# The samples' share of the last 256 features, their statistics and their output moved behind the second tokens' last product

## The chip, the cores and the metric

The kernel runs on one NeuronCore of one Trainium2 chip. The metric is the device time of one launch in microseconds (us), and a lower one is better. Engines are named as the profile names them: PE is TensorE (PEld its weight loads), DVE is VectorE, ACT is ScalarE, POOL is GpSimd, SP is SyncE, which here only issues transfers.

## The reference

One layer of a decoder trunk is computed for 256 prompt tokens and for 32 sample tokens (8 sequences of 4), with 2048 features, in float32. The part that matters here is its end: the feed-forward block, and a layer norm over the 2048 features of each token.

```python
    x = layer_norm(ALPHA * x + merged @ w_o, ln1_g, ln1_b)
    hid = jnp.square(jax.nn.relu(x @ w_up))
    x = layer_norm(ALPHA * x + hid @ w_down, ln2_g, ln2_b)

def layer_norm(x, g, b):
    xf = x.astype(jnp.float32)
    mu = jnp.mean(xf, -1, keepdims=True)
    var = jnp.mean(jnp.square(xf - mu), -1, keepdims=True)
    return ((xf - mu) * lax.rsqrt(var + LN_EPS) * g.astype(jnp.float32) + b.astype(jnp.float32)).astype(x.dtype)
```

The last `x` is written out as `y_prompt` (256 x 2048) and `y_sample` (32 x 2048).

## The kernel before

**Layout and blocks.** All activations lie with features on the 128 partitions and the 288 tokens along the free axis: columns 0 to 127 are the first prompt tokens, 128 to 255 the second, 256 to 287 the samples. A weight matrix is cut into blocks of 512 KB. For each, SP loads the block (`raw`), ACT rounds it to a high part (`hi`, L184), DVE subtracts for the low part (`lo`, L139), and PE multiplies both with the split activations (L216, L218). The loop `for i in range(len(blocks))` writes all engines' programs in one order by hand. The tile framework adds the semaphore waits between engines. Functions that belong to a block's end are hung on a later block by `at(i, f)`.

**The last 256 features.** The last product, `hid @ w_down`, adds up in `acc`. Its last 256 features (the four blocks from `mark["end"]` on) are made the other way round, with tokens on partitions: `products` (L747) writes them for the first 128 tokens into `T0[:, 256:512]` and for the second 128 into `T1`. `T0` and `T1` lie in the first halves of PSUM tiles of two times 512 columns (`acp`, two buffers). Into both, the residual is turned by products with the identity.

**The samples.** Their features are put in four groups of 32 partitions and 512 columns, `sg2`. Three quarters and more come out of `acc`: `sample_copy` (ACT, L679) gathers them, and `sample_turn` (PE, L683) turns them. The share of the last 256 features is made by `sample_products` (L701): sixteen float32 products of the samples' hidden values `hs32` with the raw weights, which leave four partial sums in a PSUM tile of its own. ACT copies them out (`s4`, L704), and one product with the constant `sel96` (L761) adds the four up in `sg2[:, 256:512]`. Then come `sample_stats` (DVE `bn_stats`, L687), four small copies that bring the groups' figures to the same 32 partitions (L714), `bn_aggr`, root, reciprocal and four copies back (`sample_means`, L726 to L730), two DVE passes over 128 x 512 (`Ys`, L142), and four transfers `y_sample` (L814). Before, `sample_products` stands ahead of the block `mark["end"] - 1`, the turning of the last groups and L761 at the start of `first_tokens`, the statistics in `late_tiles` and `sample_means`, and the `y_sample` transfers ahead of the first tokens' statistics in `final`.

**The second tokens' end.** After the last product into `T1`, PE turns three units of 512 features out of `acc` into the tiles `ws` (L841), while DVE and ACT make mean and root of the second tokens (L843 to L850). `to_rows` turns the two figures into rows (L805, L806), and `rank` (L809) adds a six-row product to each unit, so that one multiplication by 1/root finishes it. ACT does that for the units 0 and 1 (L863), DVE for unit 2 (L861). The transfers are L776: SP issues those of the units 0 and 2, ACT that of unit 1.

Of the kernel before, what the change touches and what calls it, by code (L numbers as in the profile page):

```python
# [9 lines left out]
F32 = mybir.dt.float32  # L10
# [91 lines left out]
def hybrid_kernel(ctx: ExitStack, tc: tile.TileContext, A):  # L102
# [16 lines left out]
    def nm(s):  # L119
        counter[0] += 1  # L120
        return f"{s}{counter[0]}"

    def gtile():
        n = nm("g")
        return gp.tile([P, 512], F32, tag="g", name=n)
# [15 lines left out]
    def stt(out, a, s, b, o0, o1):  # L141
        dve.scalar_tensor_tensor(out=out, in0=a, scalar=s, in1=b, op0=o0, op1=o1)  # L142
# [439 lines left out]
    def down_evac(c, p):  # L582
        def f(ps):
            a = ph["acc"][:, 2 * p:2 * p + 2, :]
            tt(a, a, ps[:, :, 0:NT], ADD)
        if c == 3:
            idle = lambda ps: None
            if p == 0:
                return [f, idle, lambda ps: out_tiles(p)]
            if p in (2, 5):  # L590
                u = p // 3
                return [f, lambda ps: out_tiles(p), lambda ps: block_stats(u, range(4)),
                        lambda ps: (block_stats(u, range(4, 8)), block_rows(u), block_moves(u, (0, 1)))] + (
                            [idle] * (3 * u)) + [lambda ps: block_moves(u, (2, 3))]
            if p == 6:
                return [f, late_tiles, lambda ps: sample_means(0), lambda ps: sample_means(1)]
            gain = lambda ps: tt(ph["Y"][:, 0, 0:512], ph["Y"][:, 0, 0:512], ph["g2"][:, 0:512], MUL)
            return [f, lambda ps: tail_rows(p // 2), lambda ps: out_tiles(p)] + [gain] * (p == 4)
        return [f]
# [81 lines left out]
    def sample_turn(w0, first):  # L681
        for w in (w0, w0 + 1):
            pe.matmul(ph["sg2"][:, w * P:w * P + P], ph["cs"][:, w * P:w * P + P], ident,  # L683
                      start=not first or w == w0, stop=not first, is_transpose=True)

    def sample_stats(u):
        dve.bn_stats(out=ph["bns"][:, u, :], in_=ph["sg2"][:, 256 * u:256 * u + 256])  # L687
# [7 lines left out]
        sample_copy(3)  # L695

    def sample_products():
        s4 = gtile()
        for k in range(KT):
            w = k % 4  # L700
            pe.matmul(s4[32 * w:32 * w + 32, 0:256], ph["hs32"][:, k, :], raw[mark["end"] + k // 4][:, w, :],  # L701
                      start=k < 4, stop=k >= KT - 4)
        ph["s4"] = ph["pool"].tile([P, 2, NT], F32, tag="yt", name="s4", bufs=2)[:, 0, 0:256]
        act.copy(ph["s4"], s4[:, 0:256])  # L704

    def late_tiles(ps):
        sample_turn(0, False)
        for u in range(2):
            sample_stats(u)
        a, sm, T0 = ph["acc"], ph["sm"], ph["T0"]  # L710
        for k in range(2):
            pe.matmul(T0[:, k * P:k * P + P], a[:, 12 + k, 0:P], ident, start=False, stop=False, is_transpose=True)
        for j in range(4):
            (act.copy if j % 2 else gps.tensor_copy)(ph["bnq"][:, j], ph["bns"][32 * j:32 * j + 32].rearrange("p k s -> p (k s)"))  # L714
        g = gtile()
        for k in range(2):
            pe.transpose(g[:, k * P:k * P + P], a[:, 12 + k, P:NP_], ident)
        dve.bn_stats(out=ph["bn"][:, 1, 8, :], in_=g[:, 0:256])
        act.copy(ph["Y"][:, 1, 1536:1792], g[:, 0:256])


    def sample_means(step):
        sm = ph["sm"]
        mq, mr = sm[0:32, 20:22], sm[:, 22:24]
        if step == 0:
            dve.bn_aggr(out=mq, in_=ph["bnq"])  # L726
            act.activation(mq[:, 1:2], mq[:, 1:2], AF.Sqrt, bias=epsc[0:32, 0:1])
            dve.reciprocal(out=mq[:, 1:2], in_=mq[:, 1:2])
            for j in range(4):
                (act.copy if j % 2 else gps.tensor_copy)(mr[32 * j:32 * j + 32], mq)  # L730
            return
        fin, bn = ph["fin"], ph["bn"]
        for b, n in ((0, 8), (1, 9)):
            dve.bn_aggr(out=fin[:, b, 1:3], in_=bn[:, b, 0:n])
            dve.tensor_scalar(out=fin[:, b, 2:3], in0=fin[:, b, 2:3], scalar1=fin[:, b, 0:1], scalar2=None, op0=MUL)
        stt(ph["Ys"], ph["sg2"], mr[:, 0:1], ph["gs"], SUB, MUL)

    kept = []

# [9 lines left out]
    def first_tokens(i, k0):  # L749
        kept.append((his.pop(i), los.pop(i)))  # L750
        a = ph["acc"]
        if k0 == 0:
            ph["T0"] = acp.tile([P, 2, 512], F32, tag="acc", name=nm("acc"))[:, 0]
            for k in range(2):
                pe.matmul(ph["T0"][:, 256 + k * P:256 + k * P + P], a[:, 14 + k, 0:P], ident,
                          start=k == 0, stop=False, is_transpose=True)
            sample_copy(0)
            sample_copy(1)
            ph["sg2"] = gtile()
            sample_turn(2, True)  # L760
            pe.matmul(ph["sg2"][:, 256:512], cst("sel96"), ph["s4"], start=False, stop=True)  # L761
        products(ph["T0"][:, 256:512], 0, k0 // KB)

    def final():
        a, fin, sm, Y, Ys = ph["acc"], ph["fin"], ph["sm"], ph["Y"], ph["Ys"]
        g2, b2 = ph["g2"], ph["b2"]
        T0 = ph["T0"]
        T1 = acp.tile([P, 2, 512], F32, tag="acc", name=nm("acc"))[:, 0, 0:256]
        for k in range(2):
            pe.matmul(T1[:, k * P:k * P + P], a[:, 14 + k, P:NP_], ident, start=k == 0, stop=False, is_transpose=True)  # L770
        for j in range(2):
# [37 lines left out]
            pe.matmul(w, ph["st5"][b], ph["m5"][:, 512 * n:512 * n + 512], start=start, stop=True)  # L809


        stt(Ys, Ys, sm[:, 23:24], ph["bs"], MUL, ADD)
        for j in range(4):
            sp.dma_start(A["y_sample"].rearrange("b t f -> (b t) f")[:, 512 * j:512 * j + 512], Ys[32 * j:32 * j + 32])  # L814

        c = slice(1536, D)
        dve.bn_stats(out=fin[:, 0, 3:9], in_=T0)
        dve.bn_aggr(out=sm[:, 0:2], in_=fin[:, 0])
# [16 lines left out]
        finish_unit(0, 0, w)  # L835
        finish_unit(0, 2)

        ws = [gtile() for _ in range(3)]
        for n, w in enumerate(ws):
            for k in range(4):  # L840
                pe.matmul(w[:, P * k:P * k + P], a[:, 4 * n + k, P:NP_], ident, start=(k == 0), stop=False,  # L841
                          is_transpose=True)
        dve.bn_stats(out=fin[:, 1, 3:9], in_=T1)  # L843
        dve.bn_aggr(out=sm[:, 2:4], in_=fin[:, 1])
        root(1)
# [1 line left out]
        high(1, mv)  # L847
        centred(1, slice(1792, D), T1)
        low(1, mv)
        dve.reciprocal(out=sm[:, 7:8], in_=sm[:, 3:4])  # L850
        for c in (slice(1792, D), slice(1536, 1792)):
            if c.start == 1536:
                centred(1, c, Y[:, 1, c])
            stt(Y[:, 1, c], Y[:, 1, c], sm[:, 7:8], b2[:, c], MUL, ADD)
            out(1, 3, c=c)
        to_rows(1)
        for n in (0, 2, 1):
            c = slice(512 * n, 512 * n + 512)
            rank(ws[n], 1, n, False)
            if n == 2:  # L860
                dve.tensor_scalar(out=Y[:, 1, c], in0=ws[n], scalar1=sm[:, 7:8], scalar2=None, op0=MUL)  # L861
            else:
                act.mul(Y[:, 1, c], ws[n], sm[:, 7:8])  # L863
            out(1, n, act if n == 1 else sp)

    mark["up"] = len(blocks)
    for c in range(4):
# [818 lines left out]
    for i in range(len(blocks)):  # L1686
# [71 lines left out]
            tail_consts()  # L1758
        if i == mark["end"] - 3:
            sample_sum()  # L1760
        if i == mark["end"] - 1:
            sample_products()
        matmuls(i)
        if i == 4:
            x_last()
# [47 lines left out]
```

## Time and profile before

| what | us |
|---|---|
| median of 3 runs (lowest, highest) | 1650.9 (1650.72, 1651.02) |
| the profiled execution, its own time | 1650.88 |
| its span, first instruction to the end of the last | 1649.1 |
| PE busy | 1642.1 |
| DVE, ACT, POOL busy | 987.3, 780.2, 136.6 |
| PE's share of the chain that ended last | 98% |

The span is what the trace shows; 1.78 us of the execution's own time lie outside it. PE is busy nearly all the time, and the chain that ended last runs through PE up to the last product into `T1`. Behind that it hops between DVE, ACT and PE, and the last transfers follow. Idle time of any other engine costs nothing by itself, unless PE or this tail waits for it.

### The profile page before, as it was taken

What the parts mean: (1) busy time and instruction counts of PE and PEld (TensorE: products, weight loads), DVE (VectorE), ACT (ScalarE), POOL (GpSimd) and SP (SyncE); (2) the same over time, 40 slices, a digit from 0 to 9 for tenths busy, and PEclk for the clock granted to TensorE, in tenths of its full rate; (3) what the DMA queues carried; (4) which work ended last, traced back from release to release, by engine and by line L of the source; (5) the groups of instructions that cost most, each with busy time, mean ns of one, the idle gap of its engine ahead of it and who ended that gap; (6) DMA issues with size and microseconds to landing.
All of it is one profiled execution on the core that took longest, in us unless ns stands there. A gap on an engine that the chain in (4) does not pass through costs nothing.

```text
span 1649.1 us, 30934 instructions
## 1 busy us (share of the span) xinstructions
PE 1642.1 (100%) x12858; PEld 1629.3 (99%) x12858; DVE 987.3 (60%) x1342; ACT 780.2 (47%) x1216; POOL 136.6 (8%) x286
## 2 busy tenths in 40 slices
PE   9999999999999999999999999999999999999998
PEld 8999999999999999999999999999999999999998
DVE  6787788878544444457776666444444444444466
ACT  7774678367533333334354454443334433344354
POOL 1132214234000000000000000000000000000111
PEclk9999999999999999999999999999999999999999
DMA  8667466846655555555565555555555555555653
GB/s 266 174 176 207 141 173 199 226 117 185 191 166 166 167 166 167 167 166 160 178 202 166 168 166 167 166 165 165 164 164 164 165 165 166 167 166 167 181 164 100
DMA packets 278999, 282.49 MB, mean 171 GB/s; under 512 B 15075, under 2 KB 272920, under 8 KB 278596
## 3 DMA queue, kind: packets, MB, share of 16 engines
q1 hardware_dynamic: 274394, 268.42, 54.2%
q0 software_dynamic: 4032, 11.63, 2.5%
q8 instruction: 101, 1.65, 0.4%
q10 hardware_dynamic: 432, 0.46, 0.1%
q14 instruction: 40, 0.33, 0.1%
HBM read 272.83 MB, written 7.63 MB: 170 GB/s over the span
## 4 chain that ended last, share of the span: by engine, by line
PE 98%; ACT 0%; DVE 0%; POOL 0%; issue 0%; ACTq 0%
PE acc L216 63%; PE acc L218 31%; PE acc L747 1%; PE g L1541 0%; PE g L1561 0%; PE g L1564 0%; PE g L1341 0%; PE g L1241 0%; PE g L1514 0%; PE g L1553 0%; PE g L1350 0%; PE g L1045 0%; PE g L701 0%; PE g L1425 0%; PE g L1402 0%; DVE lo L139 0%
## 5 line engine op out<-in xcount | busy, mean ns | idle before, releaser
L139 DVE TENSOR_TENSOR lo<-raw,hi 128x1024 fp32r<-128x1024 f32 (+1 forms) x503 | 607.1, 1210 | 561.0 <-ACT hi L184 558.6
L184 ACT CAST hi<-raw 128x1024 fp32r<-128x1024 f32 (+1 forms) x499 | 518.8, 1042 | 725.3 <-PE acc L216 637.5
L216 PE MATMUL acc<-xh,hi 128*128 128x288 f32 x1408 | 397.4, 298 | 0.0
L216 PE MATMUL acc<-xl,hi 128*128 128x288 f32 x1408 | 393.9, 295 | 0.0
L218 PE MATMUL acc<-xh,lo 128*128 128x288 f32 x1408 | 302.0, 295 | 0.1
L216 PE MATMUL acc<-dl,hi 128*128 128x288 f32 (+1 forms) x1024 | 287.7, 295 | 0.0
L216 PE MATMUL acc<-dh,hi 128*128 128x288 f32 (+1 forms) x1024 | 287.4, 295 | 0.0
L216 PE MATMUL acc<-hl,hi 128*128 128x288 f32 x992 | 277.8, 295 | 0.0
L216 PE MATMUL acc<-hh,hi 128*128 128x288 f32 x992 | 277.4, 294 | 0.0
L216 PEld LDWEIGHTS acc<-xh,hi 128*128 128x128 f32 x1408 | 264.4, 188 | 2.6 <-issue 1.3
L216 PEld LDWEIGHTS acc<-xl,hi 128*128 128x128 f32 x1408 | 264.2, 188 | 0.7
L218 PEld LDWEIGHTS acc<-xh,lo 128*128 128x128 f32 x1408 | 225.9, 188 | 0.4 <-DVE lo L139 0.3
L218 PE MATMUL acc<-dh,lo 128*128 128x288 f32 (+1 forms) x1024 | 219.8, 296 | 0.0
L218 PE MATMUL acc<-hh,lo 128*128 128x288 f32 x992 | 213.2, 296 | 0.0
L216 PEld LDWEIGHTS acc<-dh,hi 128*128 128x128 f32 x1024 | 193.3, 189 | 0.0
L216 PEld LDWEIGHTS acc<-dl,hi 128*128 128x128 f32 x1024 | 192.8, 188 | 0.0
L216 PEld LDWEIGHTS acc<-hh,hi 128*128 128x128 f32 x992 | 186.4, 188 | 0.4 <-issue 0.4
L216 PEld LDWEIGHTS acc<-hl,hi 128*128 128x128 f32 x992 | 186.1, 188 | 0.0
L218 PEld LDWEIGHTS acc<-dh,lo 128*128 128x128 f32 x1024 | 164.5, 188 | 0.0
L218 PEld LDWEIGHTS acc<-hh,lo 128*128 128x128 f32 x992 | 159.0, 188 | 0.0
L216 PE MATMUL acc<-mh,hi 128*128 128x288 f32 x256 | 71.9, 297 | 0.0
L216 PE MATMUL acc<-ml,hi 128*128 128x288 f32 x256 | 71.7, 295 | 0.0
(425 smaller groups left out, 1475.4 us busy)
## 6 DMA issues: line engine op xcount, KB each, us to landing
raw<-in_w_in_dram SPq DMA_DIRECT2D x175, 512.0 KB, 3.9
raw<-in_w_up_dram SPq DMA_DIRECT2D x128, 512.0 KB, 3.8
raw<-in_w_down_dram SPq DMA_DIRECT2D x128, 512.0 KB, 3.5
raw<-in_w_o_dram SPq DMA_DIRECT2D x32, 512.0 KB, 3.6
raw<-in_w_a_out_dram SPq DMA_DIRECT2D x16, 512.0 KB, 3.6
raw<-in_w_b_out_dram SPq DMA_DIRECT2D x16, 512.0 KB, 3.6
out_dram<-S POOLq DMA_DIRECT2D x8, 512.0 KB, 4.5
S<-in_state_gdn_dram POOLq DMA_DIRECT2D x4, 512.0 KB, 6.4
```

The source lines that it names most:

```text
L139: dve.tensor_tensor(out=out, in0=a, in1=b, op=op)
L184: act.copy(his[i][:, k:k + step], raw[i][:, k:k + step])
L216: pe.matmul(o, h[:, k, c], x, start=st and x is xh_, stop=False)
L218: pe.matmul(o, l[:, k, c], xh_, start=False, stop=en)
L747: pe.matmul(out, x[:, kk, c], w[:, k, :], start=False, stop=stop)
```

## The change

The sixteen products of the samples with the raw weights (L700 in the changed file) now follow the last product into `T1`. Their partial sums go into the second half of `T1`'s tile (`ph["s4p"]`), and `sg2` is the second half of `T0`'s tile, where both had PSUM tiles of their own. All four `sample_turn` products stand together in `late_tiles`. ACT copies the partial sums between two steps of the second tokens' statistics. The three units of the second tokens are turned one by one just ahead of their `rank`, the `sel96` product stands in unit 0, and ACT multiplies all three. The samples' statistics stand between unit 0 and unit 2, their small copies are shared by DVE and POOL instead of ACT and POOL, and the `y_sample` transfers come last.

```diff
@@ down_evac @@
             if p == 6:
-                return [f, late_tiles, lambda ps: sample_means(0), lambda ps: sample_means(1)]
+                return [f, late_tiles, lambda ps: None, lambda ps: earlier_records()]
@@ sample_products @@
-        s4 = gtile()
         for k in range(KT):
             w = k % 4
-            pe.matmul(s4[32 * w:32 * w + 32, 0:256], ph["hs32"][:, k, :], raw[mark["end"] + k // 4][:, w, :],
+            pe.matmul(ph["s4p"][32 * w:32 * w + 32], ph["hs32"][:, k, :], raw[mark["end"] + k // 4][:, w, :],
                       start=k < 4, stop=k >= KT - 4)
         ph["s4"] = ph["pool"].tile([P, 2, NT], F32, tag="yt", name="s4", bufs=2)[:, 0, 0:256]
-        act.copy(ph["s4"], s4[:, 0:256])
@@ late_tiles @@
         sample_turn(0, False)
-        for u in range(2):
-            sample_stats(u)
+        sample_turn(2, True)
+        sample_stats(0)
...
-        for j in range(4):
-            (act.copy if j % 2 else gps.tensor_copy)(ph["bnq"][:, j], ph["bns"][32 * j:32 * j + 32].rearrange("p k s -> p (k s)"))
...
-    def sample_means(step):
+    def sample_mean(step):
         sm = ph["sm"]
         mq, mr = sm[0:32, 20:22], sm[:, 22:24]
         if step == 0:
+            sample_stats(1)
+            for j in range(4):
+                (dve if j < 2 else gps).tensor_copy(ph["bnq"][:, j], ph["bns"][32 * j:32 * j + 32].rearrange("p k s -> p (k s)"))
             dve.bn_aggr(out=mq, in_=ph["bnq"])
+        elif step == 1:
             act.activation(mq[:, 1:2], mq[:, 1:2], AF.Sqrt, bias=epsc[0:32, 0:1])
             dve.reciprocal(out=mq[:, 1:2], in_=mq[:, 1:2])
             for j in range(4):
-                (act.copy if j % 2 else gps.tensor_copy)(mr[32 * j:32 * j + 32], mq)
-            return
+                (dve if j < 2 else gps).tensor_copy(mr[32 * j:32 * j + 32], mq)
+            stt(ph["Ys"], ph["sg2"], mr[:, 0:1], ph["gs"], SUB, MUL)
+            stt(ph["Ys"], ph["Ys"], mr[:, 1:2], ph["bs"], MUL, ADD)
+
+    def earlier_records():
         fin, bn = ph["fin"], ph["bn"]
...
-        stt(ph["Ys"], ph["sg2"], mr[:, 0:1], ph["gs"], SUB, MUL)
@@ first_tokens @@
-            ph["T0"] = acp.tile([P, 2, 512], F32, tag="acc", name=nm("acc"))[:, 0]
+            t0 = acp.tile([P, 2, 512], F32, tag="acc", name=nm("acc"))
+            ph["T0"], ph["sg2"] = t0[:, 0], t0[:, 1]
...
-            ph["sg2"] = gtile()
-            sample_turn(2, True)
-            pe.matmul(ph["sg2"][:, 256:512], cst("sel96"), ph["s4"], start=False, stop=True)
@@ final @@
-        T1 = acp.tile([P, 2, 512], F32, tag="acc", name=nm("acc"))[:, 0, 0:256]
+        t1 = acp.tile([P, 2, 512], F32, tag="acc", name=nm("acc"))
+        T1, ph["s4p"] = t1[:, 0, 0:256], t1[:, 1, 0:256]
...
-        stt(Ys, Ys, sm[:, 23:24], ph["bs"], MUL, ADD)
-        for j in range(4):
-            sp.dma_start(A["y_sample"].rearrange("b t f -> (b t) f")[:, 512 * j:512 * j + 512], Ys[32 * j:32 * j + 32])
...
-        ws = [gtile() for _ in range(3)]
-        for n, w in enumerate(ws):
-            for k in range(4):
-                pe.matmul(w[:, P * k:P * k + P], a[:, 4 * n + k, P:NP_], ident, start=(k == 0), stop=False,
-                          is_transpose=True)
+        sample_products()
         dve.bn_stats(out=fin[:, 1, 3:9], in_=T1)
...
         low(1, mv)
+        act.copy(ph["s4"], ph["s4p"])
+        to_rows(1)
...
-        to_rows(1)
-        for n in (0, 2, 1):
+
+        def unit(n):
+            w = gtile()
+            for k in range(4):
+                pe.matmul(w[:, P * k:P * k + P], a[:, 4 * n + k, P:NP_], ident, start=(k == 0), stop=False,
+                          is_transpose=True)
+            if n == 0:
+                pe.matmul(ph["sg2"][:, 256:512], cst("sel96"), ph["s4"], start=False, stop=True)
             c = slice(512 * n, 512 * n + 512)
-            rank(ws[n], 1, n, False)
-            if n == 2:
-                dve.tensor_scalar(out=Y[:, 1, c], in0=ws[n], scalar1=sm[:, 7:8], scalar2=None, op0=MUL)
-            else:
-                act.mul(Y[:, 1, c], ws[n], sm[:, 7:8])
+            rank(w, 1, n, False)
+            act.mul(Y[:, 1, c], w, sm[:, 7:8])
             out(1, n, act if n == 1 else sp)
+
+        unit(0)
+        sample_mean(0)
+        sample_mean(1)
+        unit(2)
+        unit(1)
+        for j in range(4):
+            sp.dma_start(A["y_sample"].rearrange("b t f -> (b t) f")[:, 512 * j:512 * j + 512], Ys[32 * j:32 * j + 32])
@@ the loop over the blocks @@
-        if i == mark["end"] - 1:
-            sample_products()
```

The order in which instructions stand, first on PE between the first and the second of the four last blocks (`acc_17693` and `acc_17674` are `T0`'s tile, `g_17698` is `sg2` before, `r` holds the gathered samples, `cf` the identity). Before:

```order
L747 MATMUL acc_17693<-hi_17545,hl_15798 128x256
L683 MATMUL g_17698<-cf,r_16693 128x128 x2
L712 MATMUL acc_17693<-cf,acc 128x128 x2
L717 MATMUL g_17724<-cf,acc 128x128 x2
L747 MATMUL acc_17693<-hi_17581,hh_15797 128x256
```

The same place in the changed kernel:

```order
L749 MATMUL acc_17674<-hi_17545,hl_15798 128x256
L683 MATMUL acc_17674<-cf,r_16693 128x128 x4
L710 MATMUL acc_17674<-cf,acc 128x128 x2
L713 MATMUL g_17698<-cf,acc 128x128 x2
L749 MATMUL acc_17674<-hi_17581,hh_15797 128x256
```

All four turned groups now stand here, and they go into the same tile as the products around them. In the built program the wait of L710 for DVE counts up to the `bn_stats` of that tile (L687); before, the wait of L712 counted up to the last addition into `acc`.

PE from the last product into `T1` on (`acc_17785` and `acc_17751` are `T1`'s tile, the three `g` tiles of L841 and L855 the units). Before:

```order
L747 MATMUL acc_17785<-hi_17688,hl_15798 128x256
L841 MATMUL g_17865<-cf,acc 128x128 x4
L841 MATMUL g_17866<-cf,acc 128x128 x4
L841 MATMUL g_17867<-cf,acc 128x128 x4
L805 MATMUL g_17892<-cf,R 6x128
L809 MATMUL g_17865<-g_16692 128x512
L809 MATMUL g_17867<-g_16692 128x512
L809 MATMUL g_17866<-g_16692 128x512
```

The changed kernel, behind the same last product:

```order
L700 MATMUL acc_17751<-raw_17446,hs_17553 32x256 x4
L700 MATMUL acc_17751<-raw_17480,hs_17553 32x256 x4
L700 MATMUL acc_17751<-raw_17511,hs_17553 32x256 x4
L700 MATMUL acc_17751<-raw_17543,hs_17553 32x256 x4
L806 MATMUL g_17850<-cf,R 6x128
L855 MATMUL g_17859<-cf,acc 128x128 x4
L858 MATMUL acc_17674<-s_17842,g_14818 128x256
L810 MATMUL g_17859<-g_16692 128x512
L855 MATMUL g_17882<-cf,acc 128x128 x4
L810 MATMUL g_17882<-g_16692 128x512
L855 MATMUL g_17890<-cf,acc 128x128 x4
L810 MATMUL g_17890<-g_16692 128x512
```

The sixteen products stand where the twelve turns stood, and the turns stand behind L806. They write `T1`'s tile, and in the built program the wait of the second tokens' `bn_stats` (L843 before, L836 now) for PE counts up to the last instruction that wrote this tile: the last L747 before, the last L700 now.

ACT from the second tokens' root (L791, now L792) on. Before:

```order
L791 ACTIVATE r_16693<-r_16693,epsc 128x1
L797 COPY R<-r_16693 128x2x2
L806 COPY g_16692<-g_17892 6x128
L863 ACTIVATE Y<-g_17865,r_16693 128x512
L863 ACTIVATE Y<-g_17866,r_16693 128x512
L776 DMA out_dram<-Y 128x512
```

The changed kernel:

```order
L792 ACTIVATE r_16693<-r_16693,epsc 128x1
L798 COPY R<-r_16693 128x2x2
L843 COPY s_17842<-acc_17751 128x256
L807 COPY g_16692<-g_17850 6x128
L861 ACTIVATE Y<-g_17859,r_16693 128x512
L727 ACTIVATE r_16693<-r_16693,epsc 32x1
L861 ACTIVATE Y<-g_17882,r_16693 128x512
L861 ACTIVATE Y<-g_17890,r_16693 128x512
L777 DMA out_dram<-Y 128x512
```

The samples' root (L727) now stands between the first and the second multiplication of the second tokens.

## The prediction

> **What bounds the kernel now.** The page comes first: the span, PE's busy share, and the chain that ended last.
>
> ```profile
> span 1649.1 us, 30934 instructions
> PE 1642.1 (100%) x12858; PEld 1629.3 (99%) x12858; DVE 987.3 (60%) x1342; ACT 780.2 (47%) x1216; POOL 136.6 (8%) x286
> PE 98%; ACT 0%; DVE 0%; POOL 0%; issue 0%; ACTq 0%
> ```
>
> PE bounds everything up to the last product into `T1`. So an instruction taken off PE ahead of that point is worth its time, and what stands behind it counts only along the tail. The second view is the chain in order of time (start, us, what), around the place that loses the sixteen products, and from the last product on.
>
> ```profile
> 1621.97 1.86 PE g L701 x32
> ...
> 1627.44 0.22 PE g L683 x2
> 1627.65 0.43 PE g L761 x2
> 1628.09 1.42 PE acc L747 x12
> 1629.51 0.22 PE g L683 x2
> 1629.72 0.22 PE acc L712 x2
> ```
>
> ```profile
> 1641.16 0.02 issue
> 1641.18 0.44 DVE r L843
> ...
> 1642.61 0.04 issue
> 1642.65 0.29 PE g L805
> ...
> 1642.96 0.26 ACT g L806
> ...
> 1643.27 0.51 PE g L809
> ...
> 1643.85 0.44 ACT Y L863
> ...
> 1644.43 0.68 ACT Y L863
> ```
>
> The reader sees a tail of 3.95 us from the last product (1641.16) to ACT's last multiplication (1645.11). I count it from S, the start of the second tokens' `bn_stats` (L843), here 1641.18: L805 starts at S+1.47 and ends at S+1.76.
>
> **The stream ahead of the last product: 2.29 us come off PE.** These are the sixteen products (1.86) and the `sel96` product (0.43). The first pair of L683 (0.22) only moves behind the twelve L747. So PE would reach the four L683 at 1629.51 - 1.86 - 0.43 - 0.22 = 1627.00. They turn what ACT copies in L679, and the timeline shows ACT and DVE there (start, us, engine, line, [idle before <- releaser]):
>
> ```profile
> 1625.03 1.44 ACT L674 COPY Y<-Y 32x192 f32<-32x192 f32 x4
> 1626.49 0.37 ACT L704 COPY s<-g 128x256 f32<-128x256 f32 x1
> 1627.03 1.05 ACT L184 CAST hi<-raw 128x1024 fp32r<-128x1024 f32 x1 [0.17 <-ACT s L704]
> 1628.05 0.50 ACT L679 COPY r<-acc 128x128 f32<-128x128 f32 x2
> ...
> 1628.11 1.23 DVE L139 TENSOR_TENSOR lo<-raw,hi 128x1024 fp32r<-128x1024 f32 x1
> 1629.76 0.76 DVE L687 BATCH_NORM_STATS2 r<-g 128x6 f32<-128x256 f32 x2 [0.42 <-PE g L683]
> ```
>
> **The stall that takes most of it back.** ACT is occupied without a gap until L674 ends at 1626.47, and nothing of that depends on PE. With L704 gone, the cast L184 starts at 1626.49 instead of 1627.03, and the two L679 end at 1626.49 + 1.52 = 1628.01. PE therefore waits from 1627.00 to about 1627.85 for the first copy and to 1628.05 for the second, and its fourth L683 is done near 1628.55. Then L710 stands behind L687, since `sg2` now shares `T0`'s tile. DVE does the subtraction L139 first: the cast ends at 1627.54, so L139 runs from 1627.57 to 1628.80, and one L687 (half of 0.76, and up to 0.43) ends near 1629.20. A released pair on PE costs 0.04 + 0.29 + 0.11, by L805's rows and the pipelined half of 0.22, so L710 is through at 1629.64; before, L712 was through at 1629.94. Of 2.29 us 0.30 are left, between 0.1 and 0.5 by how the copies overlap. The last product into `T1` ends at 1641.16 - 0.30 = 1640.86. Here PE idles in two pieces (0.85 and 0.65 us) where before it had none; all that follows it, the first tokens' end included, only moves along.
>
> **The tail: the sixteen products stand ahead of the statistics.** L700 writes into `T1`'s tile, and the `bn_stats` of the second tokens (L836) waits for the last instruction that wrote this tile. So it starts at 1640.86 + 1.86 + 0.02 = 1642.74 = S, 1.56 later than before. What was meant to lie beside the statistics lies ahead of them, and PE idles during them, while the twelve turns that lay there move behind L806 (the old L805).
>
> From there I follow the samples, since their transfers are now last. PE ends L806 at S+1.76, four turns (2 x 0.22) at S+2.20, the `sel96` product (0.43) at S+2.63. ACT's copy of the partial sums fits between its other steps, as ACT's st5 copy (L807) starts only at S+1.78. DVE is occupied longer, by the three L142 over the last 512 features:
>
> ```profile
> 1642.70 1.40 DVE L142 SCALAR_TENSOR_TENSOR Y<-Y,r,g 128x256 f32<-128x256 f32 x3
> ```
>
> That is to 1644.10 before, S+2.92. Then the second L687 ends at S+3.30. The steps that follow it are the old ones, in which DVE takes ACT's copies; the old rows time them:
>
> ```profile
> 1630.59 0.41 POOL L714 COPY r<-r 32x12 f32<-32x12 f32 x2 [3.23 <-DVE r L687]
> 1631.07 0.36 DVE L726 BATCH_NORM_AGGREGATE r<-r 32x2 f32<-32x48 f32 x1 [0.21 <-POOL r L714]
> 1631.46 0.29 ACT L727 ACTIVATE r<-r,epsc 32x1 f32<-32x1 f32 x1 [0.20 <-DVE r L726]
> 1631.79 0.15 DVE L728 RECIPROCAL r<-r 32x1 f32<-32x1 f32 x1 [0.36 <-ACT r L727]
> 1632.00 0.39 POOL L730 COPY r<-r 32x2 f32<-32x2 f32 x2 [1.01 <-DVE r L728]
> 1633.08 0.75 DVE L142 SCALAR_TENSOR_TENSOR r<-g,r,gs 128x512 f32<-128x512 f32 x1
> 1633.86 0.75 DVE L142 SCALAR_TENSOR_TENSOR r<-r,bs 128x512 f32<-128x512 f32 x1
> 1634.64 1.75 SPq L814 DMA_DIRECT2D out_dram<-r  x4
> ```
>
> L687 ended at 1629.76 + 0.76 = 1630.52 and ACT's root began at 1631.46, 0.94 later; so L727 now begins at S+4.24. From there 0.54 to POOL's copies, 0.39 for them, 0.07 to the first pass over `Ys`, 0.78 to the second and 0.75 in it: `Ys` is done at S+6.77. SP starts the first of four transfers 0.03 later (1633.86 + 0.75 to 1634.64), S+6.80, and the fourth 3/4 of 1.75 later, S+8.11 = 1650.85. All of these hops take as long as they did; none is hidden by other work now, where before PE's stream hid them all.
>
> ACT must keep program order: after unit 0's multiplication (rank at about S+3.1, done by S+3.8) comes L727, which waits for DVE until S+4.24. Units 2 and 1 are queued behind it and start only at S+4.55. The two multiplications, 1.26 us together by the old chain (1643.85 to 1645.11), end at S+5.81, and ACT issues its transfer at 1648.58. SP's transfer of unit 2 waits for such a multiplication, and the y_sample transfers stand behind it on SP, but `Ys` is later anyway. Ahead of the first tokens' transfers, where they stood, nothing waited for them: SP's first L776 came at 1637.26, 0.87 after the last had been issued (1634.64 + 1.75). Giving DVE's old multiplication to ACT costs one more 0.6 us there. Before:
>
> ```profile
> 1637.26 8.17 SPq L776 DMA_DIRECT2D out_dram<-Y  x8
> ...
> 1645.03 0.40 SPq L776 DMA_DIRECT2D out_dram<-Y  x1
> 1645.14 0.35 ACTq L776 DMA_DIRECT2D out_dram<-Y  x1
> ```
>
> **The end of the span.** How long it lasts from the last transfer I take from the windows of half a us (engines, granted clock, share of the DMA engines, GB/s), around the old `y_sample` transfers and at the end.
>
> ```profile
> 1636.50:1637.00 0.50, 0.50 (x6) 0.50 (x6) 0.50 (x2) 0.20 (x1) 0.00 (x0) 1.00 0.56 139
> 1637.00:1637.50 0.50, 0.50 (x6) 0.50 (x5) 0.50 (x3) 0.00 (x0) 0.00 (x0) 1.00 0.37 90
> ...
> 1646.50:1647.00 0.50, 0.00 (x0) 0.00 (x0) 0.00 (x0) 0.00 (x0) 0.00 (x0) 0.62 0.99 381
> ...
> 1647.50:1648.00 0.50, 0.00 (x0) 0.00 (x0) 0.00 (x0) 0.00 (x0) 0.00 (x0) 0.50 0.09 29
> ```
>
> The fourth old transfer started at 1634.64 + 1.31 = 1635.95, and the traffic stopped 0.37 / 0.56 of a half us after 1637.00, at 1637.33: 1.38 after the issue. At the end traffic stops at 1647.55, 1.55 ahead of the span's end. So now the data end at 1650.85 + 1.38 = 1652.23 and the span at 1653.8, +4.7 us. ACT's transfer alone, 3.44 us later than before, would end it at 1652.5; its 256 KB are through before the samples' last 64 KB.
>
> **Sum.** From S the old tail took 1649.10 - 1641.18 = 7.92 us, the new one takes 8.11 + 1.38 + 1.55 = 11.04. Span: 1649.10 - 0.30 (stream) + 1.86 (products in the tail) + 3.12 (the longer tail) = 1653.78. The profiled execution's own time was 1650.88, 1.78 above its span and 0.02 under the median 1650.9. So **1655.6 us**, 4.7 or 0.28% over before; 0.2%, about what a measurement can tell from no change, is 3.3 us, at 1654.2. My own bounds: the stall's rest 0.1 to 0.5; DVE's 32-partition copies instead of ACT's, from nothing to 0.3 either way (0.41 for two on POOL is the nearest row, and I take that they end beside POOL's); the transfers' end 0.3 less or 0.5 more. Together 1654.8 to 1656.6.
>
> **Rivals.** *Waits by half tile (0.08).* The two uses of each shared tile lie in different halves of 512 columns. The page "PSUM — Partial Sum Buffer" of the Trainium skill, section "PSUM bank collisions raise a hardware error", asks for a guard per bank and quadrant, and its specifications give 512 float32 values as a bank; no trace here shows it. If waits went by halves, L710 would follow the last L683 at 1628.55, 1.17 earlier than before, so `T1` would end at 1639.99 and the statistics start at S' = 1640.01, beside L700. L700 would end at 1641.85, and L806 at 1642.13, then turns and `sel96` (0.87) at 1643.00, and L687 at 1643.43 instead of S+3.30 = 1646.04. That is 2.6 less: 1653.0, not slower by the 0.2%. It decides from the place of one wait, L836's. Against it speaks the built program, where L836 counts up to the last L700 and L710 up to L687.
>
> *The early stall is smaller (0.05).* If ACT's copies came early enough, the whole 2.29 would be kept though L836 still waits for L700: 1655.6 - 2.0 = 1653.6. Against it: ACT has no gap from 1625.03 to 1628.55.
>
> *The PE clock falls (0.05).* PE's last three products before:
>
> ```profile
> 1643.27 0.96 PE L809 MATMUL g<-g 6*128 6x512 f32 x3 [0.34 <-ACT g L806]
> ```
>
> The granted clock drops to half about 2.4 us after they end at 1644.23 (0.62 in the window from 1646.50). Now PE idles 1.5 us in the tail, between L700 and L806. If it dropped there, turns and `sel96` would double (+0.87), of which DVE's S+2.92 hides 0.29: +0.6, 1656.2. The page "TensorE: Matmul & The Clock Gate" of the Trainium skill, section "What's actually happening", gives an idle window of about 3.4 us; by that the clock stays.
>
> **How the numbers follow.** Forecast 0.81, all of it above 1654.2; clock 0.05, also slower; half tiles 0.08 and small stall 0.05 within 0.2%; 0.01 is left for faster by over 0.2%, since even the half-tile case ends 2.1 us later. Slower 0.86, same 0.13, faster 0.01. The range reaches from the small stall's 1653.5 to the upper bound with the clock's price, 1657.2.
>
> **What would show it.** In the new trace: PE idle some 1.5 us around L683 and L710; L836 starting only when L700 ends, near 1642.7; DVE's L687 and ACT's L727 near 1646 and 1647, with ACT idle before L727; four y_sample transfers from about 1649.5 as the last. If L836 starts before L700 ends, or the last `T1` product ends more than a us earlier than 1641.16, the forecast is wrong.

## The result

The changed kernel takes 1655.79 us (median of 7 executions, 1655.35 to 1658.97), the kernel before 1650.88 (1650.37 to 1651.04): a ratio of 1.0035, 95% interval 1.0025 to 1.0045. It is slower by 4.9 us; 1655.6 was predicted. The profiled execution took 1657.08 us, with a span of 1655.3; it is one of those in which the granted clock fell for a while, which the others show only by their times. The four executions that by their times are without it have spans of 1653.6 to 1654.0.

The chain in order of time (start, us, what), from the early stall to the end, answers to the one shown of before:

```profile
1621.59 1.83 DVE r L660 x7
...
1624.92 0.35 ACT Y L674
...
1626.38 1.05 ACT hi L184
1627.43 0.02 issue
1627.46 1.27 DVE lo L139
1628.73 0.35 DVE r L687
1629.08 0.04 issue
1629.13 0.44 PE acc L710 x2
...
1642.25 1.91 PE acc L700 x32
1644.15 0.02 issue
1644.18 0.45 DVE r L836
...
1645.43 0.16 DVE R L139
...
1647.10 0.35 DVE r L687
...
1650.11 0.75 DVE r L142
```

Before, this chain was PE's alone in this stretch up to the last product. Now DVE and ACT set it for 7.5 us early on (from L660 at 1621.59 to the end of L687 at 1629.08), and behind L700 it runs through the samples' statistics instead of the second tokens' units. The table of PE's waits, from 1620 on (who <- whom: us in total, times, longest), names three; before, PE waited nowhere in this stretch for more than 0.34 us (ahead of L809):

```profile
PE g L806 <- DVE R L139: 1.5, 1, 1.5
PE acc L683 <- ACT r L679: 1.0, 1, 1.0
PE acc L710 <- DVE r L687: 0.7, 1, 0.7
```

The timeline of the tail gives the steps that the prediction timed (start, us, engine, line, [idle before <- releaser]):

```profile
1642.18 1.93 PE L700 MATMUL acc<-raw,hs 128*32 128x256 f32 x32
1644.18 0.43 DVE L836 BATCH_NORM_STATS2 r<-acc 128x6 f32<-128x256 f32 x1 [2.12 <-PE acc L700]
1645.64 0.27 PE L806 MATMUL g<-cf,R 128*6 128x128 f32 x1 [1.53 <-DVE R L139]
1647.02 0.42 DVE L687 BATCH_NORM_STATS2 r<-acc 128x6 f32<-128x256 f32 x1
1648.35 0.29 ACT L727 ACTIVATE r<-r,epsc 32x1 f32<-32x1 f32 x1 [0.36 <-DVE r L725]
1648.55 1.41 ACT L861 ACTIVATE Y<-g,r 128x512 f32<-128x512 f32 x2
1649.99 0.36 ACTq L777 DMA_DIRECT2D out_dram<-Y  x1
1650.11 0.75 DVE L142 SCALAR_TENSOR_TENSOR r<-r,bs 128x512 f32<-128x512 f32 x1
1650.89 1.77 SPq L870 DMA_DIRECT2D out_dram<-r  x4
```

DVE stands idle for 2.12 us until the sixteen products are through; PE then waits 1.53 for DVE; the samples' four transfers are the last thing issued.

The next view has nothing like it in the kernel before. Its rows are windows of half a us just behind the early stall (us; PE, PEld, DVE, ACT and POOL busy with their counts; granted clock; DMA share, GB/s).

```profile
1629.50:1630.00 0.50, 0.50 (x7) 0.50 (x6) 0.18 (x1) 0.00 (x0) 0.21 (x1) 1.00 0.00 0
1630.00:1630.50 0.50, 0.50 (x5) 0.50 (x4) 0.50 (x2) 0.21 (x1) 0.00 (x0) 0.52 0.00 0
...
1633.00:1633.50 0.50, 0.50 (x4) 0.50 (x4) 0.00 (x0) 0.00 (x0) 0.00 (x0) 0.56 0.00 0
1633.50:1634.00 0.50, 0.50 (x7) 0.50 (x6) 0.00 (x0) 0.00 (x0) 0.00 (x0) 1.00 0.00 0
```

For 3.4 us the clock is at half and PE, busy throughout, gets 4 or 5 products done in half a us instead of 7.

### The profile page after: what moved, and what is told of

The parts are those of the page before. It is cut to its first block, busy times and chain, and to the rows that moved or that the text cites. A ratio compares the mean times of both kernels' runs of the same rounds, so it can differ in the third digit from the quotient of the medians.

```text
span 1655.3 us, 30932 instructions
## 1 busy us (share of the span) xinstructions
PE 1644.7 (99%) x12858; PEld 1630.9 (99%) x12858; DVE 987.2 (60%) x1345; ACT 779.8 (47%) x1213; POOL 137.8 (8%) x286
## 4 chain that ended last, share of the span: by engine, by line
PE 97%; DVE 1%; ACT 0%; issue 0%; POOL 0%; POOLq 0%
PE acc L216 62%; PE acc L218 31%; PE acc L749 1%; PE g L1547 0%; PE g L1567 0%; PE g L1570 0%; PE g L1347 0%; PE g L1247 0%; PE g L1520 0%; PE g L1559 0%; PE g L1356 0%; DVE lo L139 0%; PE g L1051 0%; ACT hi L184 0%; PE acc L700 0%
```

## The experiments

All times are medians; the kernel before ran beside each group and gave 1650.69, 1650.67 and 1650.53.

**The halves exchanged.** `sg2` goes to `T1`'s tile and the products to `T0`'s.

```diff
@@ late_tiles @@
+        t1 = acp.tile([P, 2, 512], F32, tag="acc", name=nm("acc"))
+        ph["T1"], ph["sg2"] = t1[:, 0, 0:256], t1[:, 1]
...
-            ph["T0"], ph["sg2"] = t0[:, 0], t0[:, 1]
+            ph["T0"], ph["s4p"] = t0[:, 0], t0[:, 1, 0:256]
...
-        t1 = acp.tile([P, 2, 512], F32, tag="acc", name=nm("acc"))
-        T1, ph["s4p"] = t1[:, 0, 0:256], t1[:, 1, 0:256]
+        T1 = ph["T1"]
```

> The two second halves are exchanged: the samples' projections (sg2) lie in the second half of T1's tile, and the products of the last 256 features (s4p) in the second half of T0's tile. With that the products on T0 follow nothing of VectorE's in their tile, and VectorE's statistics of T1 follow nothing of the sample products in theirs. Theory (a wait counts to the last writer of the whole tile, though the halves are disjoint): both waits go. The L710 pair no longer ends behind the second half of the statistics (1.3 us of PE stream come back until the next wait, ScalarE's L679, sets it), and the second tokens' statistics start about 1.9 us earlier than in the changed kernel, straight behind T1's last product: 1652.5 to 1653.5, middle 1653.0, against 1655.7 of the changed kernel. Rival (the waits go by half already, or the time is that of the work and not of the waits): no difference, 1655.3 to 1656.0. Second rival (the tail's end is set by the sample chain from the products' end, not from the statistics): the chain then starts behind L700 anyway and 1654.5 to 1655.5 remains.

1652.73 us (1652.43 to 1653.44, 11 executions), 3.06 under the changed kernel. The statistics now start beside the products, 0.10 behind the first of them, and the pair that waited for L687 (now L712) follows L683 at once:

```profile
1627.11 0.75 PE L683 MATMUL acc<-cf,r 128*128 128x128 f32 x4 [1.00 <-ACT r L679]
1627.70 0.38 PE L712 MATMUL acc<-cf,acc 128*128 128x128 f32 x2
...
1639.19 1.93 PE L700 MATMUL acc<-raw,hs 128*32 128x256 f32 x32
1639.29 0.43 DVE L837 BATCH_NORM_STATS2 r<-acc 128x6 f32<-128x256 f32 x1 [0.22 <-PE acc L751]
```

No instruction was added or removed, so about 3 of the 4.9 us lay in which half shares a tile with which (3.1 by the medians, 2.9 with each taken over the kernel before beside it). The theory of waits by whole tile holds; both rivals fall. PE's wait at L683 (1.00) is still there, and no execution stands out as three of the changed kernel's do.

**A tile of its own for the products**, which takes only the tail's wait away.

```diff
-        T1, ph["s4p"] = t1[:, 0, 0:256], t1[:, 1, 0:256]
+        T1 = t1[:, 0, 0:256]
...
+        ph["s4p"] = gtile()[:, 0:256]
         sample_products()
```

> The products of the last 256 features go to a tile of their own; sg2 stays in T0's tile. Theory: only the tail's wait goes, VectorE's statistics of T1 run beside the products (1.86 us) and the chain behind them starts that much sooner; the early wait of the L710 pair on L687 stays. 1653.7 to 1654.3, middle 1654.0. Rival (the wait is not what costs in the tail; PE's own work behind T1 is): PE does the 1.86 us of products between T1's last product and the turns in both cases, so no difference, 1655.3 to 1656.0. If the halving of the granted clock behind the early stall comes from PE's idle time there, single executions still show it, since the early stall is left in.

1654.56 (1653.45 to 1656.71, 8 executions), where 1653.7 to 1654.3 was expected. Four lie near the forecast, at 1653.45 to 1654.09, 1.8 under the changed kernel's undisturbed ones; four lie at 1655.0 to 1656.7. The profiled one, of the second sort (1655.34), has the statistics beside the products again (DVE waits 0.22, for L749), the two early gaps, and the half clock behind them. That the other three long ones have the fall too is inferred from their times and their mean clocks (the granted clock over the whole span: 0.998 in the four long ones, 0.999 in the four short ones).

**The products back where they were.**

```diff
-        T1, ph["s4p"] = t1[:, 0, 0:256], t1[:, 1, 0:256]
+        T1 = t1[:, 0, 0:256]
...
-        sample_products()
...
-        act.copy(ph["s4"], ph["s4p"])
...
+        if i == mark["end"] - 1:
+            ph["s4p"] = gtile()[:, 0:256]
+            sample_products()
+            act.copy(ph["s4"], ph["s4p"])
```

> The 32 sample products and ScalarE's copy of them stand where they stood in the kernel before, ahead of the last block but one's end, in a tile of their own; all else is as in the changed kernel (statistics, Ys and transfers behind the second tokens' last product, the turns one unit at a time, three units by ScalarE). Theory: moving the products brought almost nothing (the stall took 1.99 of 2.29 us back), so putting them back costs 0.3 us ahead of T1's end and takes the 1.86 us out of the tail: 1653.8 to 1654.6, middle 1654.3. Rival (the sample share's statistics and transfers at the end cost nothing beyond the 1.86 us): 1651 to 1652. What is left over 1650.9 here is the price of the statistics, their two later multiplications and the four transfers behind S.

1654.21 (1653.78 to 1654.64): the forecast. Moving the products cost 1.6 us where it was to gain; 3.5 stay with the samples' statistics and transfers and the units. PE still waits for L687 (0.53), but not for L679, and no execution stands out: with this one early gap the clock did not fall.

**ACT's copies first.** In the last full block the split of the weights stands behind the products and copies.

```diff
-        if i > 5:
+        if i > 5 and i != mark["end"]:
...
+        if i == mark["end"]:
+            split_hi(i + ahead)
```

(VectorE's part of the split moves likewise, behind `late_tiles`.)

> In the last full block ScalarE's part of the next weights' split (1.44 us, L674 and L184) stands behind the block's products, so that its two copies for the samples (L679) come first, and VectorE's part of that split stands behind the samples' first statistics. Theory: PE's wait at L683 (0.75 us in the changed kernel) and most of that at L710 (0.70) go; about 1.2 us come off ahead of T1's end: 1654.0 to 1654.9, middle 1654.5. And if the fall of the granted clock to half for 3.4 us follows from those two gaps in PE's work, no execution has it: single times within 0.5 us of each other. Rival (the split is then late for the products on T0 and T1, and takes it back): 1655.3 to 1656.5. Rival on the clock (the fall has nothing to do with the gaps): single times still spread over 2 to 3 us.

1654.38 (1653.94 to 1654.95): the forecast, though the single times spread over 1.0 us where 0.5 was expected. The wait at L683 is gone (it was 1.00 in the changed kernel; the 0.75 of the expectation is how long these turns take), the one at L710 is 0.53, and the clock of the profiled execution stays at 1.00 in this stretch. This trace also prices the fall. The same work, from L710 to PE's turns at L771 and to the statistics L836, first in the changed kernel:

```profile
1629.13 0.44 PE L710 MATMUL acc<-cf,acc 128*128 128x128 f32 x2 [0.70 <-DVE r L687]
...
1635.42 0.38 PE L771 MATMUL acc<-cf,acc 128*128 128x128 f32 x2
```

then here:

```profile
1627.98 0.44 PE L710 MATMUL acc<-cf,acc 128*128 128x128 f32 x2 [0.53 <-DVE r L687]
...
1632.76 0.38 PE L771 MATMUL acc<-cf,acc 128*128 128x128 f32 x2
...
1641.51 0.43 DVE L836 BATCH_NORM_STATS2 r<-acc 128x6 f32<-128x256 f32 x1 [2.12 <-PE acc L700]
```

6.29 against 4.78 us: the fall costs 1.51. From L771 on both need the same (8.76 and 8.75).

**Both edits together** (halves exchanged, copies first).

> The exchanged halves of the first experiment and the copies put first of the fourth together: no wait at L683 and L710 and none of the statistics for the sample products. Theory: what is left of the early stall in the first experiment is PE's 1.0 us at L683, and that goes; the tail stays at 11.4 us behind the second tokens' last product: 1651.3 to 1652.1, middle 1651.7. It would still lie 1.0 us behind the kernel before, whose tail is 7.9 us long. Rival (both edits free the same time, so they do not add): 1652.5 to 1652.9.

1652.29 (1651.61 to 1652.72), between the theory and the rival, 0.44 under the first experiment where 1.0 was expected. By the traces the stretch from the first tokens' turns (L760) to the statistics went from 14.99 (1624.30 to 1639.29) to 14.05 us (1625.31 to 1639.36), so 0.94 did go; but this execution reached L760 1.0 later, and the kernels' arrival there varies by that much (1624.26 to 1625.31 in this study). With both early waits and the statistics' wait gone, the change still loses 1.6 us by the medians; the interval of the ratio, 0.9999 to 1.0017, just reaches no difference.

**The units alone**: the kernel before, with one part of the change.

```diff
-        ws = [gtile() for _ in range(3)]
-        for n, w in enumerate(ws):
-            ... four turns each ...
...
-            rank(ws[n], 1, n, False)
-            ... DVE multiplies unit 2, ACT the others ...
+            w = gtile()
+            ... four turns ...
+            rank(w, 1, n, False)
+            act.mul(Y[:, 1, c], w, sm[:, 7:8])
```

> The kernel before with one part of the change alone: the twelve turns stand behind the second tokens' moments, one unit at a time, and ScalarE multiplies all three units (before: the turns run during the statistics, and VectorE multiplies one unit). Theory: the first rank product starts 0.44 us later and ScalarE's third multiplication ends at about 1646.1 in place of 1645.1, and the last transfer follows it: 1651.5 to 1652.1, middle 1651.9, against 1650.8. Rival (the last transfer waits for the queue of the earlier ones anyway): no difference, 1650.4 to 1651.0. If the theory holds, this part is 1.0 of the 4.9 us.

1652.41, more than expected, and wide (1651.51 to 1653.11). The profiled execution (1651.6) shows the 0.9 that the order explains: from the statistics on 8.83 us (1640.97 to 1649.8), before 7.92. The next run asks what the others lose beyond that.

**The units alone, with PE kept busy.** Twelve turns of the identity stand where the old turns were.

```diff
+        filler = gtile()
+        for _ in range(12):
+            pe.transpose(filler[:, 0:P], ident, ident)
         dve.bn_stats(out=fin[:, 1, 3:9], in_=T1)
```

> The kernel with the units part alone (turns behind the moments, one unit at a time, three multiplications by ScalarE) took 1652.41 with single times from 1651.5 to 1653.1, where the order of its work explains 0.9 us over the kernel before. Here twelve turns of the identity into a tile of their own stand where the twelve turns were: PE is busy during the second tokens' statistics, as before, and the fillers' results are not used. Theory (with PE idle for 1.6 us there, the granted clock falls for part of the tail in some executions): the spread shrinks and the median goes to 1651.4 to 1651.9. Rival (the spread is that of the last transfer): 1652.2 to 1652.6, the same spread.

1651.56 (1651.13 to 1651.98), as expected. PE's idle time during the statistics is filled, and 0.85 us are gone by the medians (0.7 with each taken over the kernel before beside it), although work was added. In the traces the wait at L805 goes from the first row to the second:

```profile
1642.53 0.27 PE L805 MATMUL g<-cf,R 128*6 128x128 f32 x1 [1.60 <-DVE r L845]
```

```profile
1642.49 0.27 PE L805 MATMUL g<-cf,R 128*6 128x128 f32 x1 [0.20 <-DVE R L139]
```

So this part is 0.9 us by its order, and on the median 0.7 to 0.85 more that goes when PE is kept busy. That the second is the clock fits the mean clocks of whole executions (0.998 in the seven longer ones, 0.999 to 1.0 in the four shorter; with the fillers never under 0.999), but no trace of a longer one of these exists, so it is not shown.

**Fillers in the early waits** of the changed kernel.

```diff
+        filler = gtile()
+        for _ in range(8):
+            pe.transpose(filler[:, 0:P], ident, ident)
         sample_turn(0, False)
         sample_turn(2, True)
         sample_stats(0)
+        for _ in range(6):
+            pe.transpose(filler[:, 0:P], ident, ident)
```

> The changed kernel, with both early waits left as they are, and PE kept busy in them: eight turns of the identity into a tile of their own stand ahead of the L683 turns, six ahead of the L710 pair. They compute nothing that is used. Theory (the granted clock falls to half for 3.4 us because PE idles 1.0 and 0.7 us within one such window): no execution shows the fall, and single times lie within 0.6 us, between 1655.0 and 1655.8. The fillers may end a little behind the waits, so the median can lie up to 0.6 us above the 1655.4 of the undisturbed executions. Rival (the fall has another cause than PE's idling, as ScalarE's or VectorE's load there): the fall stays in about half of the executions, spread 1655.3 to 1659.

1655.77 (1654.95 to 1656.41, 6 executions). The profiled one has the clock at 1.00 throughout the stretch, and none reaches the 1657 to 1659 of the changed kernel, but the spread is 1.5, where 0.6 was expected, and the median is unchanged. The mean clock is 0.997 in two of the six, as in the two other long ones of the changed kernel. By an estimate that is half clock for over 8 us (0.0025 of 1654 us is 4.1 us lost at half the rate), and behind PE's last product only 6.0 us are left in the profiled execution (1647.2 to 1653.2). So in these two the clock seems to have been low while PE worked, at a place that no trace shows, and this run does not settle it.

**The gap made longer.**

```diff
-        sample_copy(2)
+        for _ in range(5):
+            sample_copy(2)
```

> The changed kernel with the first early wait made longer: ScalarE does the copy of the samples' third quarter five times in place of once (0.25 us each), so that PE waits 1.0 us more at L683. Theory (PE idling 1.7 us within one window of 3.4 us is just enough for the granted clock to fall, which is why only some executions of the changed kernel show it; with 2.7 us of idling all do): the profile shows the clock at half for 3.4 us behind the gap, and the time is 1655.4 plus 1.0 for the copies plus 1.7 for the clock: 1657.5 to 1658.7 in nearly all executions. Rival (the fall is a matter of chance and not of the idle time): about half the executions at 1656.4, half at 1658.

1659.05, over the 1657.5 to 1658.7 expected: four of five executions at 1658.18 to 1659.6, one at 1656.53 with a mean clock of 0.999 (0.995 to 0.997 in the others). The profile shows the longer wait and two windows' length of half clock:

```profile
1628.57 1.10 PE L683 MATMUL acc<-cf,r 128*128 128x128 f32 x4 [2.31 <-ACT r L679]
```

```profile
1628.00:1628.50 0.50, 0.00 (x0) 0.00 (x0) 0.15 (x1) 0.50 (x3) 0.46 (x2) 1.00 0.00 0
1628.50:1629.00 0.50, 0.43 (x2) 0.39 (x3) 0.50 (x1) 0.22 (x2) 0.46 (x2) 0.63 0.00 0
1629.00:1632.00 3.00, 2.48 (x13) 2.08 (x12) 1.70 (x4) 0.18 (x1) 1.50 (x3) 0.50 0.00 0
1632.00:1635.00 3.00, 3.00 (x16) 3.00 (x16) 0.79 (x4) 1.58 (x5) 0.00 (x0) 0.50 0.00 0
1635.00:1635.50 0.50, 0.50 (x4) 0.50 (x4) 0.00 (x0) 0.00 (x0) 0.00 (x0) 0.54 0.00 0
```

From 1628.63 (0.63 of the second row) to 1635.46 (0.54 of the last) it is 6.83 us, twice the 3.4 of the changed kernel, and the median rose by 3.3 for 1.3 us of longer waiting. In this execution the clock is at half once more, from 1649.11 on, with 3.5 us of PE's work still ahead. The row of ACT's last multiplication shows what that costs:

```profile
1652.66 0.69 ACT L862 ACTIVATE Y<-g,r 128x512 f32<-128x512 f32 x1 [1.08 <-PE g L811]
```

It ends 7.27 us behind the start of the statistics (1646.08), where it ended 5.78 behind it in the changed kernel. The span ends 11.62 instead of 11.12 behind it, and `Ys` is done at the same 6.7. So part of what this execution lost lies in the tail.

Longer idling goes with a fall in more executions. ACT's four more copies came with it, so this run alone does not part the two; that ACT's same work in another order (copies first) shows no fall speaks for the idle time. That one execution escaped shows that something besides, which the program does not set, has a part in it.

**Can the end be shortened?** Two kernels build on both edits: the samples' output in one transfer, or in four from three queues.

```diff
-        for j in range(4):
-            sp.dma_start(A["y_sample"].rearrange("b t f -> (b t) f")[:, 512 * j:512 * j + 512], Ys[32 * j:32 * j + 32])
+        sp.dma_start(A["y_sample"].rearrange("b t (j f) -> j (b t) f", j=4), Ys)
```

> As the combined kernel before it in this list, with the samples' output in one transfer of 128 rows in place of four of 32. Theory (the end is set by SP issuing four transfers in a row, 0.44 us each, behind Ys): three of them go, 1.3 us, and the kernel ends 0.4 us under the kernel before: 1650.0 to 1650.8, middle 1650.4. Rival (the end is set by bytes still queued from the second tokens' output, or one transfer of 256 KB lands later than four of 64 KB): 1651.3 to 1652.1, no difference from the combined kernel.

1654.5 (1654.18 to 1654.84), 2.2 slower: neither theory. The windows show why: the single transfer keeps about a quarter of the DMA engines' time busy (shares of 0.18 to 0.29) at 29 to 100 GB/s, for four us, where four transfers run at a share of 0.54 and 131 GB/s and stop 2.7 us behind `Ys` (1649.0, with `Ys` done at 1646.26). First with one transfer, in windows of one us, then with four, in windows of half a us:

```profile
1647.00:1648.00 1.00, 0.00 (x0) 0.00 (x0) 0.00 (x0) 0.00 (x0) 0.00 (x0) 0.50 0.29 29
...
1650.00:1651.00 1.00, 0.00 (x0) 0.00 (x0) 0.00 (x0) 0.00 (x0) 0.00 (x0) 0.50 0.26 100
```

```profile
1648.00:1648.50 0.50, 0.00 (x0) 0.00 (x0) 0.00 (x0) 0.00 (x0) 0.00 (x0) 0.50 0.54 131
1648.50:1649.00 0.50, 0.00 (x0) 0.00 (x0) 0.00 (x0) 0.00 (x0) 0.00 (x0) 0.50 0.53 131
1649.00:1649.50 0.50, 0.00 (x0) 0.00 (x0) 0.00 (x0) 0.00 (x0) 0.00 (x0) 0.50 0.00 0
```

The page "DMA: Bandwidth & Descriptors" of the Trainium skill, section "Why a DMA increments its semaphore by 16 and not by 1", says that a transfer is spread over the largest number of engines up to 16 that divides the outermost size on both sides. That is 4 for this view (4 x 32 x 512) and 16 for each of the four (32 x 512); a share of 0.26 agrees with 4 of 16.

The other variant issues the four in turn from SP, ACT, SP and POOL:

```diff
-            sp.dma_start(A["y_sample"].rearrange("b t f -> (b t) f")[:, 512 * j:512 * j + 512], Ys[32 * j:32 * j + 32])
+            (sp, act, sp, gps)[j].dma_start(A["y_sample"].rearrange("b t f -> (b t) f")[:, 512 * j:512 * j + 512], Ys[32 * j:32 * j + 32])
```

> The combined kernel (halves exchanged, copies first; 1652.29) with the samples' four transfers issued from three queues: two by SP, one each by ScalarE and GpSimd; the one transfer of 128 rows tried before took 2.2 us more and is given up. Theory (SP's issuing, 0.44 us each, sets the end): the last leaves 0.9 us earlier, 1651.2 to 1651.7, still above the kernel before. Rival (bytes set the end: the second tokens' units and the samples' 256 KB share the same engines): 1652.0 to 1652.5.

1651.87 (1651.59 to 1652.45), between the theory and the rival. It is 0.42 better by the medians, and 0.3 with each taken over the kernel before beside it; the single times of the two overlap over most of their range, so what the queues bring is not settled. It is still 1.3 above the kernel before. No version here beats that kernel, and the traces give a reason. PE needs the same time for `T1`'s products and the sixteen sample products in either order. The combined kernel's tail lasts 9.5 us behind the sample products (L700 ends at 1641.18, the span at 1650.7), the old one 7.9 behind `T1`'s last product. With the sample products last on PE, the longer of the two chains starts last, so they belong ahead. That is worked out from these rows; no version was tried that keeps these edits and puts the products ahead.

## Why the prediction was right, point by point

- *The early stall takes most of 2.29 us back*: right. Forecast were waits of 0.85 us at L683 and 0.65 at L710; measured 1.00 and 0.70. With the clock's 1.51 taken off, the statistics start at 1644.18 - 1.51 = 1642.67; forecast 1642.74. With ACT's copies first, which takes the wait at L683 away and leaves 0.53 at L710, the median is 1.4 lower.
- *L836 waits for L700, by the tile and not by its half*: right; 2.12 us of waiting, and exchanging the halves or giving the products a tile of their own removes it. The waits of this program go by whole tiles, so the rival falls; its 1653.0 is about what the exchange brought (1652.73).
- *The tail from S*: right to 0.1 up to the transfers. Forecast and measured, from S = 1644.18: L687's end 3.30 and 3.26, L727 4.24 and 4.17, `Ys` 6.77 and 6.68, SP's first transfer 6.80 and 6.71, the span's end 11.04 and 11.1.
- *ACT behind L727*: right; its transfer was issued 5.81 behind S, where the multiplications were to end, and the samples' are later.
- *The early stall smaller*: did not happen; moving the copies brings it about, at 1654.4, where 1653.6 was put for it. 0.53 us at L710 remain then, as DVE is still late.
- *The clock falls*: the step that failed. It was put in the tail alone, at +0.6 us and with a chance of 0.05. It fell behind the early stall, where the prediction had seen 1.5 us of gaps and priced only the gaps, and there it cost 1.51 in the profiled execution. By their times 3 of 7 executions had it (1656.95 to 1658.97). That the median lies among the other four, and so close to the sum, is luck: with one more such execution it would be about 1657, above the prediction's own bound of 1656.6. In the tail, where PE idles for 1.53, this trace has no fall before PE's last product is done. The trace of the longer gap has one there, and its tail is 0.5 longer. That is near the 0.6 put for it, but it comes through the units' multiplications and ACT's transfer, not through the samples' chain.

By parts: the products' move costs 1.6, with the waits at L683 and L836 that go when it is undone, and the units cost 0.9 by their order. The waits by shared tiles (L710 and L836) are 3.1, and all that the edits could mend is 3.5 of the 4.9 us. The parts do not add: the same waits are counted in more than one of them, and the samples' chain and the units lie beside each other in the tail.

## What to carry to other kernels

In this program a wait counts to the last writer of a tile, not of the part that is read. Before two uses share one, ask who writes it last and who reads it: exchanging two halves was worth 3 us here. Moving work into an engine's idle time gains only if what that engine waits for does not itself wait for the moved work, and if no long chain starts behind it. Here DVE's statistics waited for the sample products, and the chain behind these is the longer one (9.5 against 7.9 us), so it should start first. Price a gap in PE's work with what the clock may take behind it as well, and look at the spread of the times: three of seven executions stood more than 1 us above the rest.

## What was not expected of the hardware

The granted clock fell to half for 3.4 us though PE had been idle only 1.0 and 0.7 us in the 3.4 us ahead. In the changed kernel's trace the first of these windows ends where the fall begins, the second is the fall, the third holds the tail's gap of 1.53, and the fourth, at full clock, follows it:

```profile
1626.61:1630.02 3.41, 1.71 (x13) 1.35 (x13) 1.81 (x3) 1.22 (x3) 2.89 (x6) 1.00 0.00 0
1630.02:1633.44 3.42, 3.42 (x19) 3.42 (x18) 1.24 (x5) 1.77 (x5) 0.00 (x0) 0.50 0.00 0
1643.67:1647.09 3.42, 1.89 (x18) 0.92 (x8) 2.70 (x9) 1.11 (x4) 0.00 (x0) 1.00 0.05 13
1647.09:1650.50 3.41, 2.15 (x11) 1.20 (x10) 2.64 (x10) 2.24 (x4) 0.74 (x4) 1.00 0.54 200
```

In the trace of the longer gap a window of the tail with the same busy time as the third has a fall behind it:

```profile
1645.70:1649.11 3.41, 1.88 (x17) 0.99 (x10) 2.82 (x9) 1.12 (x4) 0.00 (x0) 1.00 0.06 18
1649.11:1652.52 3.41, 3.41 (x11) 1.90 (x10) 2.65 (x9) 1.67 (x3) 0.73 (x4) 0.50 0.41 148
```

So PE's busy time in such a window does not decide alone. The moments at which the clock changes, worked out from the mean clock of the windows around them, lie on a grid. In the first trace they are 1630.02, 1633.44 and 1650.50 (behind PE's last product), one and five times 3.41 us apart; in the second 1628.63, 1635.46 and 1649.11, two and four times. Where a gap falls in that grid differs from execution to execution, which may be why only some have the fall; this is not shown.

The Trainium skill, "TensorE: Matmul & The Clock Gate", section "What's actually happening", has a clock that drops after an idle window of about 3.4 us, a window that runs freely. The grid, and that the fall comes in some executions only, agree with such windows; that PE must be idle for a whole one does not. One early wait of 1.0 (halves exchanged) or of 0.53 us (products back) brought no execution that stands out. Two of 1.7 together did in 3 of 7 and, with the products in a tile of their own, in 4 of 8; two of about 2.8 together in 4 of 5. Where the limit lies, and why not every execution has it, stays open.

Second, the one transfer of 128 rows kept the DMA engines at work until 5.4 us behind `Ys`, twice as long as four of 32 rows (its last window with traffic ends at 1651.5, at a share of 0.11; `Ys` was done at 1645.80).
